# RWKV-7 chunk systems: the scales go into the inverse itself, and the groups of systems are regrouped

## The chip, the cores and the metric

The kernel runs on one core of one Trainium2 chip. The metric is the device time of one execution in microseconds, the median of several runs. TensorE (PE, with its weight loads as PEld), VectorE (DVE), ScalarE (ACT) and GpSimd (POOL) each work off their own queue of instructions in order, and SyncE (SP) issues all DMAs from one queue, also in order.

## The reference, cut to what matters

Two layers run over 1104 token rows (64 sample rows and 1040 prompt rows): a gated DeltaNet layer, then an RWKV-7 layer. The change touches the RWKV-7 layer only, whose state update is

```python
kk = l2norm((k * k_k).reshape(B, T, H, N))
b_h = kk * a_h
S = (S * d_t[:, :, None, :]
     + jnp.einsum('bhvk,bhk->bhv', S, -kk_t)[..., None] * b_t[:, :, None, :]
     + v_t[..., None] * k_t[:, :, None, :])
```

The kernel computes it in chunks of 64 rows. Within a chunk the steps form a unit lower triangular system of 64 x 64, and its inverse is needed for every chunk and head. With the keys not normalised, the system is I + L D, where the diagonal D holds 1 / |key|^2 (plus 1e-6) of each row. What is stored for the later stage is D times the inverse, transposed as the matmuls need it.

## The kernel before, in words

Layer 0 comes first; its inverses of 8 groups also go through `inverse32` (72 partitions, diagonal of ones). Layer 1 has three parts: `keys_decay_rate` projects keys, decay and rate and stores them in DRAM (cakd); then `layer1` loops over 24 weight tiles (r, v and z; `project`) while the systems are inverted; then the wave, which runs the recurrence.

There are 24 items (a pair of heads by a segment of 384 columns), six chunks in each. `rwkv_inverse(b)` is called five times, within the loop behind the tiles 0, 3, 6, 9 and 12. It first prepares its items one by one (L1246 to L1291): the load of cakd into sldcak, ScalarE, VectorE and POOL scaling it, the store of abd, 24 small matmuls for the system (fL), copied by ScalarE into the diagonal blocks GD (L1274) and the lower left block L21 (L1276), and the squared norms (frss), transposed by VectorE (L1290) with 1e-6 added (L1291) into rk. Then come, for the whole group at once: the reciprocal (L1294), its transposition (bblk, L1296), the transposition of GD into invA (L1299) and its multiplication by bblk (L1300). `inverse32` eliminates 31 times, with two VectorE instructions each (L448 and L450), on a tile invT that POOL has set to the unit matrix (L442 and L443). Two transpositions make T1n (L1306) and the upper half of sTD (L1307). All of this has the same size whatever the count of items in the group.

Then `inverse_merge` runs for each item: 12 matmuls on either half of the partitions (mY: L21 by T1n), VectorE multiplying the result by rk on its way out of PSUM into invY (L465, two instructions), 12 matmuls on either half (mU), and ScalarE writing the negated result into sTD (L62). POOL multiplies the item's part of sTD by rk (L1312), and six DMAs (L1315 and L1317) write it to ttd in DRAM. Of these six, two write zeros: the upper right quarter of each inverse, which is zero from a memset at the first group (L1305).

The wave loads the inverse of an item with one DMA of 128 x 384 (rTT, L1331), when it prepares that item.

The framework arranges the instructions of this stage on all engines by a simulated timeline, so a change of one instruction shifts others past each other; in the wave only TensorE's order is written out by hand. Projections have the tile d on TensorE; their weights come by DMA (wraw), ScalarE makes whi (L86), POOL makes wlo (L90). The mixed inputs of the projections are xa, xc, xh and xl (ScalarE, VectorE and POOL).

Of the kernel before, what the change touches and what calls it, by code (L numbers as in the profile page):

```python
# [35 lines left out]
class Builder:  # L36
# [401 lines left out]
    def inverse32(self, A, nb, pool):  # L438
# [4 lines left out]
        nc.gpsimd.memset(T[:, 0:1024:33], 1.0)  # L443
# [8 lines left out]

    def inverse_merge(self, L21, TT, T1n, scale_col, pool, th0, n):

        nc = self.nc
        pY = self.ps("m", 2, "Y")
        yv = pY[:, 0:32 * n].rearrange("p (c i) -> p c i", i=32)
        for c in range(n):
            for p in (0, 1):
                a = 64 * p  # L460
                self.mm(yv[a + 32:a + 64, c, :], L21[a:a + 32, th0 + c, :], T1n[a:a + 32, th0 + c, :])
        Y = self.t(pool, [128, 192], "invY", 2)[:, 0:32 * n].rearrange("p (c i) -> p c i", i=32)
        for p in (0, 1):
            a = 64 * p + 32
            nc.vector.tensor_tensor(Y[a:a + 32], yv[a:a + 32],  # L465
                                    scale_col[a:a + 32].unsqueeze(2).broadcast_to([32, n, 32]), op=ALU.mult)
        pU = self.ps("m", 2, "U")
        uv = pU[:, 0:32 * n].rearrange("p (c i) -> p c i", i=32)
        for c in range(n):
            for p in (0, 1):  # L470
                a = 64 * p
                self.mm(uv[a:a + 32, c, :], Y[a + 32:a + 64, c, :], TT[a + 32:a + 64, c, 0, :])
        for p in (0, 1):
            a = 64 * p
            self.act(TT[a:a + 32, :, 1, :], uv[a:a + 32], AF.Identity, scale=-1.0)


# [681 lines left out]
    def rwkv_masks(self, ap, first=False):  # L1159
# [14 lines left out]
        if first:  # L1174
# [11 lines left out]
            nc.gpsimd.memset(self.GD[:, :, 30:32], 0.0)  # L1186
# [18 lines left out]
    def rwkv_open(self):  # L1205
# [4 lines left out]
        self.ttd, self.abd = self.dram([24, 128, 384], "ttd"), self.dram([24, 128, 768], "abd")  # L1210
# [28 lines left out]
    def rwkv_inverse(self, b, pool):  # L1239

        items = range(5 * b, min(5 * b + 5, 24))
        nc, t = self.nc, self.t
        rk2, L21, GD, TD = self.rk2[:, b], self.L21[b % 2], self.GD, self.TD
        for q, n in enumerate(items):
# [46 lines left out]
            nc.vector.tensor_scalar(rk2[:, C], nt[:, :, 0], 1e-6, None, op0=ALU.add)  # L1291
        if len(items) < 5:
            nc.gpsimd.memset(GD[:, :, 6 * len(items):30], 0.0)
# [14 lines left out]
        for q, n in enumerate(items):  # L1308
# [5 lines left out]
            for a in (0, 64):  # L1314
                nc.sync.dma_start(d[a:a + 32], TT[a:a + 32])  # L1315
                for x in (0, 1):
                    nc.sync.dma_start(d[a + 32:a + 64, :, x], TT[a + 32:a + 64, :, 1 - x])  # L1317
# [639 lines left out]
```

## Time and profile before

| what | us |
|---|---|
| median of three runs (2352.32 to 2361.63) | 2361.1 |
| the profiled execution | 2359.64 |
| its span | 2357.9 |
| its mean granted TensorE clock | 0.967 |
| first load of an item (sldcak) | 1471.0 |
| first mY of the first group | 1571.7 |
| first mY of the last group | 1817.2 |
| last write of ttd is issued | 1844.4 |

All places are us from the start of the span. A row of groups gives line, engine, operation, tiles written and read, shapes and count, then the busy time, the mean ns of one, and the idle time of the engine ahead of it with what ended that. A row of waits gives the waiting instruction, what it waited for, and the sum, the count and the longest. L90 and L62 are helpers' lines, so the tile names matter there. A line number in the profile is one of the kernel before; the changed kernel's numbers differ by a few.

### The profile page before, as it was taken

The numbers are of one execution on the slowest core, as the hardware profiler recorded it, in microseconds if no ns is written. First come the engines' busy times: TensorE is split into PE (matmuls) and PEld (weight loads), VectorE is DVE, ScalarE is ACT, GpSimd is POOL, SyncE is SP. The second block draws the span as 40 slices with busy tenths as digits, with TensorE's granted clock in tenths as the row PEclk, the third lists the DMA queues.
The fourth block names the chain that finished last, engine by engine and source line by source line (L and its number), as shares of the span: only waits on it lengthen the run. The fifth ranks groups of instructions, "written<-read, shape, count | busy, mean of one in ns | idle before, by whom it ended". The sixth has DMA issues, their size and how long they took to land. (4 is left out here: it accounts for less than half of the span.)

```text
span 2357.9 us, 55429 instructions
## 1 busy us (share of the span) xinstructions
PE 2159.2 (92%) x20452; PEld 1959.9 (83%) x20452; DVE 1592.9 (68%) x4248; ACT 1284.4 (54%) x3642; POOL 932.5 (40%) x1268
## 2 busy tenths in 40 slices
PE   6989999999999999999999999888888998899886
PEld 5888988888898989888989999777778876678775
DVE  6868678685867686784335833589988366667755
ACT  5455646564655555557333745647435355577763
POOL 3435334443434343344231623535334433344433
PEclk9999999999999999999999999999899999999998
DMA  3424333323333333336153154554543655677654
GB/s 113 106 69 111 88 85 81 107 66 102 90 90 94 88 112 88 84 97 194 49 160 86 46 178 161 164 152 133 172 113 89 188 151 144 178 218 227 212 161 129
DMA packets 434744, 293.37 MB, mean 124 GB/s; under 512 B 148729, under 2 KB 417642, under 8 KB 434474
## 3 DMA queue, kind: packets, MB, share of 16 engines
q1 hardware_dynamic: 434474, 289.84, 42.6%
q8 instruction: 161, 2.64, 0.5%
q14 instruction: 109, 0.89, 0.1%
HBM read 202.74 MB, written 87.00 MB: 123 GB/s over the span
## 5 line engine op out<-in xcount | busy, mean ns | idle before, releaser
L90 POOL TENSOR_TENSOR wlo<-wraw,whi 128x512 fp32r<-128x512 f32 (+2 forms) x252 | 329.6, 1310 | 351.0 <-ACT whi L86 325.8
L76 PE MATMUL d<-xc,whi 128*128 128x384 f32 (+2 forms) x910 | 261.7, 344 | 7.6 <-DVE xc L90 2.6
L86 ACT CAST whi<-wraw 128x512 fp32r<-128x512 f32 (+2 forms) x252 | 151.7, 603 | 128.9 <-PE dq L76 50.5
L415 DVE SCALAR_TENSOR_TENSOR cvy<-raw,cw,cvy 128x408 f32<-128x408 f32 (+2 forms) x288 | 178.3, 632 | 15.8 <-ACT cvy L62 13.9
L448 DVE TENSOR_TENSOR invtmp<-invA,invT 72x31 f32<-72x31 f32 (+31 forms) x403 | 173.2, 430 | 11.1 <-DMA invA<-ltd 5.1
L76 PEld LDWEIGHTS d<-xc,whi 128*128 128x128 f32 (+1 forms) x910 | 168.6, 192 | 14.3 <-issue 3.2
L450 DVE TENSOR_TENSOR invT<-invT,invtmp 72x31 f32<-72x31 f32 (+31 forms) x403 | 169.7, 421 | 6.5
L76 PE MATMUL dz<-xc,whi 128*128 128x384 f32 (+1 forms) x480 | 149.5, 343 | 0.0
L76 PE MATMUL d<-xa,whi 128*128 128x384 f32 (+3 forms) x450 | 143.0, 350 | 4.2 <-DVE xa L90 1.7
L76 PE MATMUL dv<-xc,whi 128*128 128x384 f32 (+1 forms) x480 | 146.7, 334 | 0.0
L76 PE MATMUL d<-xc,wlo 128*128 128x384 f32 (+2 forms) x428 | 142.7, 342 | 1.4 <-POOL wlo L90 1.3
L815 POOL TENSOR_SCALAR Sb<-Sb,eglb 128x128 f32<-128x128 f32 x128 | 80.4, 646 | 89.2 <-DMA Sb<-in_state_gdn 34.1
L76 PE MATMUL dv<-xa,whi 128*128 128x384 f32 (+1 forms) x288 | 100.3, 348 | 0.1
L76 PE MATMUL dz<-xa,whi 128*128 128x384 f32 (+1 forms) x288 | 100.3, 348 | 0.0
L76 PEld LDWEIGHTS d<-xa,whi 128*128 128x128 f32 (+1 forms) x450 | 83.7, 191 | 10.9 <-issue 2.7
L76 PEld LDWEIGHTS dz<-xc,whi 128*128 128x128 f32 x480 | 89.6, 192 | 0.8
L76 PEld LDWEIGHTS dv<-xc,whi 128*128 128x128 f32 x480 | 88.6, 188 | 0.5 <-issue 0.4
L76 PE MATMUL d<-xa,wlo 128*128 128x384 f32 (+3 forms) x252 | 86.7, 344 | 2.1 <-POOL wlo L90 2.1
L76 PE MATMUL d<-xh,whi 128*128 128x384 f32 (+1 forms) x256 | 84.1, 343 | 4.1 <-ACT xh L86 4.0
L62 ACT ACTIVATE o<-rA,gcol 128x128 f32<-128x128 f32 x128 | 46.6, 372 | 72.5 <-DVE S L726 72.0
L76 PE MATMUL d<-xl,whi 128*128 128x384 f32 (+1 forms) x256 | 84.0, 345 | 2.1 <-DVE xl L90 2.0
L76 PE MATMUL d<-xh,wlo 128*128 128x384 f32 (+1 forms) x256 | 83.8, 342 | 1.7 <-POOL wlo L90 1.7
(512 smaller groups left out, 7025.6 us busy)
## 6 DMA issues: line engine op xcount, KB each, us to landing
wraw<-in_gdn_w_in SPq DMA_DIRECT2D x96, 256.0 KB
wraw<-in_rwkv_w_rkvz SPq DMA_DIRECT2D x80, 256.0 KB
Sb<-in_state_gdn SPq DMA_DIRECT2D x64, 256.0 KB
sldcak<-cakd SPq DMA_DIRECT2D x24, 576.0 KB
fldcak<-cakd SPq DMA_DIRECT2D x24, 576.0 KB
cakd<-ev SPq DMA_DIRECT2D x56, 192.0 KB
wraw<-in_rwkv_w_o SPq DMA_DIRECT2D x40, 256.0 KB
E<-drow SPq DMA_DIRECT2D x24, 384.0 KB
```

The source lines that it names most:

```text
L62: return self.nc.scalar.activation(out, in_, func, bias=bias, scale=scale, **kw)
L76: self.nc.tensor.matmul(out, lhsT, rhs, start=start, stop=stop)
L86: nc.scalar.copy(hi, x)
L90: e.tensor_tensor(lo, x, hi.bitcast(F32), op=ALU.subtract)
L415: nc.vector.scalar_tensor_tensor(y[:, 0:wd], raw[:, k:k + wd], cw[k], y[:, 0:wd], op0=ALU.mult, op1=ALU.add)
L448: nc.vector.tensor_tensor(tmp, A[:, j, j + 1:32].unsqueeze(2).broadcast_to([nb, n, m]), Tv[:, j, 0:m].unsqueeze(1).broadcast_to([nb, n, m] ...
L450: nc.vector.tensor_tensor(Tv[:, j + 1:32, 0:m], Tv[:, j + 1:32, 0:m], tmp, op=ALU.subtract)
L815: nc.gpsimd.tensor_scalar(Sb[:, u], Sb[:, u], self.eglb[:, hv, 4 * g + u:4 * g + u + 1], None, op0=ALU.mult)
```

## The change

The diagonal D goes into the start of the elimination: POOL copies bblk to the diagonal of invT where ones stood, so that the inverse comes out already scaled, and nothing has to be scaled afterwards. So the VectorE multiplication of invY becomes a plain copy on ScalarE, and POOL's multiplication of sTD is gone. The addition of 1e-6 goes from VectorE to POOL. The groups are 4, 5, 5, 5 and 5 items where they were 5, 5, 5, 5 and 4; the calls stay at the same tiles. The writes of ttd, six per item, become six per group, in a DRAM tile laid out by group.

```diff
-    def inverse32(self, A, nb, pool):
+    def inverse32(self, A, nb, pool, diag=None):
...
-        nc.gpsimd.memset(T[:, 0:1024:33], 1.0)
+        if diag is None:
+            nc.gpsimd.memset(T[:, 0:1024:33], 1.0)
+        else:
+            nc.gpsimd.tensor_copy(T[:, 0:1024:33], diag)
...
-        for p in (0, 1):
-            a = 64 * p + 32
-            nc.vector.tensor_tensor(Y[a:a + 32], yv[a:a + 32],
-                                    scale_col[a:a + 32].unsqueeze(2).broadcast_to([32, n, 32]), op=ALU.mult)
+        for a in (32, 96):
+            self.nc.scalar.copy(Y[a:a + 32], v[a:a + 32])
...
-            nc.gpsimd.memset(self.GD[:, :, 30:32], 0.0)
+            nc.gpsimd.memset(self.GD[:, :, 24:32], 0.0)
...
-        self.ttd, self.abd = self.dram([24, 128, 384], "ttd"), self.dram([24, 128, 768], "abd")
+        self.ttd, self.abd = self.dram([5, 128, 1920], "ttd"), self.dram([24, 128, 768], "abd")
...
-        items = range(5 * b, min(5 * b + 5, 24))
+        items = range(max(5 * b - 1, 0), 5 * b + 4)
...
-            nc.vector.tensor_scalar(rk2[:, C], nt[:, :, 0], 1e-6, None, op0=ALU.add)
-        if len(items) < 5:
-            nc.gpsimd.memset(GD[:, :, 6 * len(items):30], 0.0)
+            nc.gpsimd.tensor_scalar(rk2[:, C], nt[:, :, 0], 1e-6, None, op0=ALU.add)
...
-        Tv = self.inverse32(A.rearrange("p i s -> p s i"), 128, pool)
+        Tv = self.inverse32(A.rearrange("p i s -> p s i"), 128, pool, blk)
...
-        for q, n in enumerate(items):
-            TT = TD[:, 6 * q:6 * q + 6]
-            self.inverse_merge(L21, TT, T1n, rk2[:, 6 * q:6 * q + 6], pool, 6 * q, 6)
-            v = TT.rearrange("p c x i -> p c (x i)")
-            nc.gpsimd.tensor_tensor(v, v, rk2[:, 6 * q:6 * q + 6].unsqueeze(2).broadcast_to([128, 6, 64]), op=ALU.mult)
-            d = self.ttd[n].rearrange("p (c x i) -> p c x i", x=2, i=32)
-            for a in (0, 64):
-                nc.sync.dma_start(d[a:a + 32], TT[a:a + 32])
-                for x in (0, 1):
-                    nc.sync.dma_start(d[a + 32:a + 64, :, x], TT[a + 32:a + 64, :, 1 - x])
+        for q in range(len(items)):
+            C = slice(6 * q, 6 * q + 6)
+            self.merge_right(self.merge_left(L21[:, C], T1n[:, C], pool), TD[:, C])
+        w = 6 * len(items)
+        d = self.ttd[b].rearrange("s (c x i) -> s c x i", x=2, i=32)[:, 0:w]
+        for a in (0, 64):
+            nc.sync.dma_start(d[a:a + 32], TD[a:a + 32, 0:w])
+            for x in (0, 1):
+                nc.sync.dma_start(d[a + 32:a + 64, :, x], TD[a + 32:a + 64, 0:w, 1 - x])
```

`merge_left` holds the mY matmuls and the copy, `merge_right` the mU matmuls and the negated write to sTD; both are otherwise the old `inverse_merge`. The wave's load of rTT takes its 384 columns out of the group's 1920. Up to the first load of an item the order of the instructions is the same on every engine, and in the wave TensorE's order is the same too.

The order shows the change at three places. First VectorE, behind the first elimination of all, where the first group is merged. Before:

```order
L1307 STREAM_TRANSPOSE sTD_18165<-invT_18669 128x32x32
L1264 TENSOR_TENSOR sldcak_19407<-sldcak_19407 128x384
L1258 TENSOR_TENSOR sldcak_19455<-sldcak_19455 128x383
L465 TENSOR_TENSOR invY_18783<-mY_18770,rk_3193_18162 32x192 x2
L1299 STREAM_TRANSPOSE invA_19503<-sGD_18164 128x1024
L1290 STREAM_TRANSPOSE rkc_19497<-frss_19492 128x192
L465 TENSOR_TENSOR invY_18821<-mY_18808,rk_3193_18162 32x192 x2
L1291 TENSOR_SCALAR rk_3193_18162<-rkc_19497 128x6
L1264 TENSOR_TENSOR sldcak_19455<-sldcak_19455 128x384
L1294 RECIPROCAL rk_3193_18162<-rk_3193_18162 128x32
L1296 STREAM_TRANSPOSE bblk_19501<-rk_3193_18162 128x32
L1300 TENSOR_TENSOR invA_19503<-invA_19503,bblk_19501 128x1024
```

The same place on VectorE with the change:

```order
L1305 STREAM_TRANSPOSE sTD_18165<-invT_18617 128x32x32
L1258 TENSOR_TENSOR sldcak_19295<-sldcak_19295 128x383
L1290 STREAM_TRANSPOSE rkc_19341<-frss_19336 128x192
L1264 TENSOR_TENSOR sldcak_19295<-sldcak_19295 128x384
L1258 TENSOR_TENSOR sldcak_19347<-sldcak_19347 128x383
L1297 STREAM_TRANSPOSE invA_19395<-sGD_18164 128x1024
L1290 STREAM_TRANSPOSE rkc_19389<-frss_19384 128x192
L1264 TENSOR_TENSOR sldcak_19347<-sldcak_19347 128x384
L1292 RECIPROCAL rk_3193_18162<-rk_3193_18162 128x32
L1294 STREAM_TRANSPOSE bblk_19393<-rk_3193_18162 128x32
L1298 TENSOR_TENSOR invA_19395<-invA_19395,bblk_19393 128x1024
L1258 TENSOR_TENSOR sldcak_19949<-sldcak_19949 128x383
```

The invY rows and the addition into rk are gone from VectorE, and its reciprocal now follows an addition on POOL. In both orders the last two items of the second group are prepared here.

Second SP, at the start of the stage, where the first two items have just been loaded. Before:

```order
L1221 DMA sldcak_18406<-cakd 128x3x384
L1150 DMA cakd<-ev_18143 128x336
L1110 DMA rvd<-ev_18342 128x384
L1110 DMA rvd<-ev_18370 128x384
L1265 DMA abd<-sldcak_18401 128x768
L1221 DMA sldcak_18458<-cakd 128x3x384
```

The same place on SP with the change:

```order
L1110 DMA rvd<-ev_18342 128x384
L1314 DMA ttd<-sTD_18165 32x24x32
L1314 DMA ttd<-sTD_18165 960x1x32
L1314 DMA ttd<-sTD_18165 32x24x32
L1314 DMA ttd<-sTD_18165 960x1x32 x7
L1110 DMA rvd<-ev_18370 128x384
```

The ten writes of zeros, two for each of the five groups, have moved ahead of the whole stage. The other writes of ttd stand behind each group's merges, in two pairs.

Third TensorE, at the first merge of the last group (mY), among projections (d). Before:

```order
L76 MATMUL d_22959<-xc_107,whi_22949 128x384 x2
L76 MATMUL d_22959<-xc_107,wlo_22950 128x384
L76 MATMUL mY_22161<-T1n_22158,L_3196_18166 32x32 x12
L76 MATMUL d_22959<-xc_107,whi_22949 128x384 x2
L76 MATMUL d_22959<-xc_107,wlo_22950 128x384
```

The same place on TensorE with the change:

```order
L76 MATMUL d_22820<-xl_2814_15536,whi_22816 128x384
L76 MATMUL d_22849<-xc_107,wlo_22811 128x384
L76 MATMUL d_22849<-xc_107,whi_22810 128x384 x2
L76 MATMUL mY_22013<-T1n_22010,L_3196_18166 32x32 x12
L76 MATMUL d_22849<-xc_107,wlo_22811 128x384
```

Here mY stands later among the projections: 232 of their matmuls came behind it, up to the first one of the wave's gate (zz), and 206 come now.

36 lines of the change are left out of this document (17 added, 19 removed).

## The prediction

> **What bounds the kernel now.** I read the page first, then the busy time in stretches, then the waits of TensorE in the stretch that the change touches. The page's head says which engine is the fullest.
>
> ```profile
> span 2357.9 us, 55429 instructions
> ...
> PE 2159.2 (92%) x20452; PEld 1959.9 (83%) x20452; DVE 1592.9 (68%) x4248; ACT 1284.4 (54%) x3642; POOL 932.5 (40%) x1268
> ```
>
> TensorE (PE) is busy 92% of the span, so anything that does not make TensorE wait less, or run at a higher clock, is worth nothing. The edits lie in one stage: the systems are inverted while the r, v and z projections run. The stretches around it (columns: PE, PEld, DVE, ACT and POOL busy us with counts, granted clock, DMA share, GB/s):
>
> ```profile
> 1420.00:1473.00 53.00, 50.68 (x286) 48.97 (x284) 22.07 (x31) 31.07 (x66) 17.40 (x22) 0.97 0.47 157
> 1473.00:1500.00 27.00, 21.23 (x135) 16.80 (x135) 17.99 (x30) 21.27 (x49) 16.92 (x27) 0.81 0.35 115
> 1500.00:1540.00 40.00, 38.72 (x471) 35.72 (x470) 20.05 (x37) 21.20 (x52) 17.61 (x36) 1.00 0.60 185
> 1540.00:1680.00 140.00, 118.29 (x1569) 104.37 (x1568) 128.85 (x271) 76.06 (x185) 59.98 (x68) 0.91 0.49 143
> 1680.00:1817.00 137.00, 118.93 (x1399) 106.81 (x1397) 126.73 (x248) 63.01 (x146) 57.86 (x56) 0.95 0.43 123
> 1817.00:1864.00 47.00, 46.81 (x427) 45.63 (x428) 16.60 (x32) 14.99 (x33) 19.21 (x37) 0.96 0.67 197
> ```
>
> From 1540 to 1817 VectorE (DVE) is busy 128.85 + 126.73 = 255.6 of 277 us, or 92%, and TensorE only 237.2: it idles 39.8 us and is granted a clock of 0.91 and 0.95. Before and behind that stretch DVE is half empty and TensorE full. So here DVE is the bound, or very near it. The waits of TensorE in that stretch say the same (us in total, times, longest):
>
> ```profile
> PE mY L76 <- DVE T1n L1306: 7.1, 4, 2.0
> PE fL L76 <- DVE sldcak L1264: 6.1, 4, 1.9
> PE d L76 <- POOL wlo L90: 3.4, 4, 1.2
> PE mU L76 <- DVE invY L465: 3.2, 3, 1.1
> ...
> PE d L76 <- DVE xc L90: 2.6, 1, 2.6
> ...
> PE fL L76 <- DVE invtmp L448: 2.4, 1, 2.4
> ...
> PE d L76 <- DVE xl L90: 2.0, 2, 1.2
> ...
> PE fL L76 <- DVE invT L450: 0.4, 1, 0.4
> ```
>
> The seven rows that name DVE hold 7.1 + 6.1 + 3.2 + 2.6 + 2.4 + 2.0 + 0.4 = 23.8 us, that is 0.60 of the 39.8 us. That share is my rate of exchange below: of a microsecond taken off DVE here, TensorE gets 0.60 back. It is the choice that matters most; its ends are 0 (the chain goes through ScalarE or the DMAs instead) and 1 (DVE alone sets the pace).
>
> **What leaves DVE.** Two groups of instructions go to other engines. In 1540 to 1817 (busy us, mean ns, idle before):
>
> ```profile
> L465 DVE TENSOR_TENSOR invY<-mY,rk 32x192 f32<-32x192 f32 x40 | 14.3, 357 | 5.7 <-PE mY L76 4.6
> ...
> L1291 DVE TENSOR_SCALAR rk<-rkc 128x6 f32<-128x6 f32 x19 | 5.7, 300 | 0.1
> ```
>
> That is 14.3 + 5.7 = 20.0 us. The 31 elimination steps are neither fewer nor shorter: a group of four items costs as much as one of five.
>
> **What leaves POOL, and what that is to DVE.** The multiplication of the finished blocks (L1312) is gone: 24 instructions in the whole stage.
>
> ```profile
> L1312 POOL TENSOR_TENSOR sTD<-sTD,rk 128x384 f32<-128x384 f32 x24 | 21.6, 899 | 55.8 <-ACT sTD L62 45.8 <-DMA ttd<-sTD 7.1 <-DMA sldcak<-cakd 2.8
> ...
> L1259 POOL COPY sldcak<-sldcak 128x6 f32<-128x6 f32 x24 | 6.4, 268 | 58.0 <-DVE sldcak L1258 51.9 <-DVE invtmp L448 5.6 <-POOL m_blocks L1179 0.5
> ```
>
> POOL is under half full, so its 21.6 us alone buy nothing. But DVE is stretched beside it: of each shape here, one instruction beside an L1312 and one without.
>
> ```profile
> 1590.43 0.83 POOL L1312 TENSOR_TENSOR sTD<-sTD,rk 128x384 f32<-128x384 f32 x1 [3.91 <-ACT sTD L62]
> ...
> 1595.64 0.98 POOL L1312 TENSOR_TENSOR sTD<-sTD,rk 128x384 f32<-128x384 f32 x1
> ```
> ```profile
> 1590.88 0.60 DVE L450 TENSOR_TENSOR invT<-invT,invtmp 128x192 f32<-128x192 f32 x1
> ...
> 1595.96 0.92 DVE L448 TENSOR_TENSOR invtmp<-invA,invT 128x240 f32<-128x240 f32 x1
> ```
> ```profile
> 1562.89 0.36 DVE L450 TENSOR_TENSOR invT<-invT,invtmp 128x192 f32<-128x192 f32 x1
> ...
> 1613.18 0.41 DVE L448 TENSOR_TENSOR invtmp<-invA,invT 128x240 f32<-128x240 f32 x1
> ```
>
> The stretch is 0.60 - 0.36 = 0.24 and 0.92 - 0.41 = 0.51, 0.37 us on the mean. With 40 invY in the stretch there are 20 such multiplications: 20 x 0.37 = 7.4 us. The ends are 0 and 20 x 0.899 = 18.0 us. *By the Trainium skill ("SBUF — State Buffer", section "Who interferes with whom") a VectorE instruction with two SBUF inputs and a GpSimd instruction that reads SBUF exclude each other for the whole instruction, which would return up to the 18.0 us and give an estimate near 2335 us. The two rows agree that there is a stall, but show only about half of it.*
>
> **What is added.** POOL gets the 24 additions of 1e-6 (128x6; the POOL copy of that shape, L1259, takes 268 ns) and the five diagonals: 6.4 + 1.3 us against 21.6 removed. New is that DVE now waits for POOL twice in a group: its reciprocal for the last addition, and its first elimination step for the copied diagonal. Behind DVE's waiting instruction stands the whole elimination. Each wait is bounded by 0 and by one POOL weight split ahead in the queue (L90 takes 1.34 us at 1592.10, quoted below); the second is covered by the 128x1024 multiplication between the transposed scales and the first step. Of 10 such waits I take 3 us in all; the ends are 0 and 13.
>
> ```profile
> 1592.10 1.34 POOL L90 TENSOR_TENSOR wlo<-wraw,whi 128x512 fp32r<-128x512 f32 x1 [0.84 <-ACT whi L86]
> ```
>
> ScalarE (ACT) gets the 48 copies out of PSUM. It has such a copy already, and the second half of each merge:
>
> ```profile
> L62 ACT ACTIVATE sTD<-mU 32x192 f32<-32x192 f32 x48 | 15.4, 320 | 23.1 <-PE mU L76 22.8
> ...
> L1276 ACT COPY L<-fL 32x192 f32<-32x192 f32 x48 | 14.8, 307 | 0.4
> ```
>
> At 307 ns they are 14.7 us; ACT is busy 139 of the 277 us, so I cost them at nothing. Their cover is that free half. The hop from mY to mU gets no longer (2 x 0.307 against 2 x 0.357). If the cover fails, see the third rival.
>
> **SP and the DMAs.** 144 writes of ttd become 30. Ten of them are the zero quarters, which no longer wait for any merge: the order puts them ahead of everything, at about 1473, in a place where SP stands still now.
>
> ```profile
> 1473.01 10.17 SPq L1110 DMA_DIRECT2D rvd<-ev  x2
> ...
> 1494.63 0.52 SPq L1221 DMA_DIRECT2D sldcak<-cakd  x1
> 1495.25 1.01 SPq L198 DMA_DIRECT2D wraw<-in_rwkv_w_rkvz  x1
> ```
> ```profile
> L1317 SPq DMA_DIRECT2D ttd<-sTD x96: 549/596/1477, 1581.4 to 1844.4; - x96
> L1315 SPq DMA_DIRECT2D ttd<-sTD x48: 308/537/879, 1580.9 to 1843.2; - x48
> ```
>
> A write of 192 runs takes SP 0.596 us, one of 32 runs 0.537, and the load at 1494.63 of 384 runs 0.52: the count of runs does not show. Ten are then 6 us within the wait of 10, and free. SP loses about 144 x 0.58 - 30 x 0.6 = 66 us of issuing, but I credit nothing: TensorE waits for a weight split on POOL only 3.4 us in the stretch. The bytes and runs are the same.
>
> **The tail.** Behind the first mY of the last group stand 232 projection matmuls in the old order and 206 in the new, so once DVE has the last transposed inverse, less is left. TensorE starts one each 0.176 us (nine single ones in a row, the first and the last: 1.41 us for eight steps):
>
> ```profile
> 1859.06 0.34 PE L76 MATMUL d<-xh,whi 128*128 128x384 f32 x1
> ...
> 1860.47 0.34 PE L76 MATMUL d<-xl,whi 128*128 128x384 f32 x1
> ```
>
> 26 x 0.176 = 4.6 us less, and one more item to merge. The tail has 47 us, of which 232 x 0.176 = 40.8 are projections; the other 6.2 us for four items make about 1.5 each at most, 1.1 if the lower clock takes its part. So -4.6 + 1.1 = -3.5 us.
>
> **The sum.** Off DVE come 20.0 + 7.4 - 3.0 = 24.4 us; at 0.60 that is 14.6 us for TensorE. With the tail: 14.6 + 3.5 = 18.1 us. The profiled execution took 2359.6 us, 1.7 more than its span, and lies 1.5 under the median of the three runs (2361.1), inside their spread. 2359.6 - 18.1 = **2341.5 us**. The head (groups of four, then fives) I cost at nothing: TensorE is 38.72 of 40 us full while the first group is prepared.
>
> **The rivals.**
> - *DVE alone sets the pace, and the clock follows.* The whole 24.4 us come off, and the waits that vanish spare slow periods too:
>
> ```profile
> 1573.00:1577.00 4.00, 2.83 (x60) 1.89 (x61) 3.58 (x7) 1.53 (x5) 2.67 (x5) 0.79 0.56 160
> 1577.00:1582.00 5.00, 5.00 (x58) 4.50 (x58) 3.05 (x8) 1.49 (x4) 1.83 (x2) 0.50 0.84 264
> ```
>
>   Right behind the first group's waits TensorE has a clock of 0.50 for 5 us, a loss of 2.5 us. With two such periods gone: 24.4 + 3.5 + 5 = 32.9, 2326.7 us. For it: DVE at 92%. Against: 16.0 us of TensorE's idle time is not DVE's. *The Trainium skill ("TensorE: Matmul & The Clock Gate", "What's actually happening") puts the drop to half clock behind an idle window of about 3.4 us; by that rule shorter waits would leave the clock alone and the sum stay as it is. The trace differs: the longest wait in the stretch is 2.6 us, and the clock halves.* Chance 0.14.
> - *The wait stays and only its name changes.* The last elimination still ends when TensorE has no other work placed ahead, since the order places mY anew. Then only the wait for invY (3.2 us) and the tail (3.5) are saved: 2353 us. Chance 0.20.
> - *ScalarE becomes the in-order blocker; slower.* It now stands twice in each merge behind TensorE's small matmuls. Today the one place costs it 22.8 us of waiting (row of sTD above); a second like it is 22.8 more, behind which stand the weight casts, the evictions of d and the mixing. If all of it reaches TensorE: + 22.8 - 3.2 - 3.5 = + 16.1, 2375.7 us. It decides from the point where such a wait is longer than ScalarE's free time around it, and that is 277 - 139 = 138 us for the 20 items of the stretch, 6.9 us each. Against: 22.8 / 24 is under 1 us. Chance 0.12.
> - *The change does not do what it says at the head*: the ten zero writes, each with 768 or 960 runs, take SP in proportion, 5 x 0.596 = 3 us each. 30 us against a gap of 10 hold the third sldcak load and the weights 20 us: 2361 us. Against: the rows of 384 runs. Chance 0.06.
>
> **How the numbers follow.** Forecast 0.48 (its own range 2332 to 2349), larger gain 0.14: faster by over 0.5% 0.62. Within 0.5%, about what a measurement of this kernel can tell from no change, 0.26 (second and fourth rival). Slower 0.12. The range runs from 2320, near the end of the larger gain with the POOL stall at its upper end, to 2363, which holds the rivals without a gain and leaves the slower one out.
>
> **What would show it.** Right: DVE busy falls by about 25 us from 1540 on with the counts of invY and rk gone from it; the last mY comes 12 to 20 us earlier; TensorE's waits for DVE shrink from 23.8 to about 10 us. Wrong: waits of TensorE on ScalarE (whi, xh, invY) in their place; DVE waiting for rk or the diagonal by more than 1 us a group; a gap on TensorE between 1485 and 1540 with SP busy on ttd. If DVE shrinks as said and the end does not move, my 0.60 was wrong.

## The result, and the profile after

The changed kernel takes 2352.45 us (median) where the kernel before takes 2361.14. The ratio is 0.9969, 95% interval 0.9956 to 0.9983: 7.3 us faster, 4.0 to 10.4. The forecast was 18.1 us, so the direction was right and the gain less than half. Below, a ratio is always to the kernel before, and times and differences go by it (the two medians alone lie 8.7 us apart); 0.001 is 2.36 us, and a range behind a difference of two kernels combines their two intervals (root of the sum of squares).

The page's head, changed kernel (profiled execution 2353.39 us):

```profile
span 2351.5 us, 55207 instructions
...
PE 2157.2 (92%) x20452; PEld 1959.8 (83%) x20452; DVE 1570.0 (67%) x4176; ACT 1298.2 (55%) x3690; POOL 922.5 (39%) x1267
```

VectorE lost 22.9 us of 1592.9, ScalarE gained 13.8, POOL lost 10. Of the stretches that the prediction showed, the four up to the last merges, now of the changed kernel:

```profile
1473.00:1500.00 27.00, 20.42 (x124) 16.48 (x124) 18.83 (x31) 21.41 (x46) 16.64 (x28) 0.87 0.61 153
1500.00:1540.00 40.00, 40.00 (x443) 37.51 (x442) 25.21 (x44) 23.30 (x57) 20.85 (x38) 1.00 0.60 187
1540.00:1680.00 140.00, 124.45 (x1639) 112.03 (x1638) 125.05 (x246) 85.51 (x211) 62.31 (x81) 0.95 0.51 157
1680.00:1817.00 137.00, 116.01 (x1402) 104.93 (x1402) 111.73 (x210) 69.12 (x167) 49.34 (x51) 0.94 0.39 114
```

In 1540 to 1817 VectorE is busy 125.05 + 111.73 = 236.8 us, 18.8 less than before: the relief came. TensorE was busy 237.2 us there and is now 240.5: it idles 36.5 us where it idled 39.8. VectorE idles 40.2 us there where it idled 21.4, and TensorE got 3.3 us of that.

A fixed stretch cuts the two kernels at different points of their work, so the measure from here on is the whole stage, from the first load of an item to the first matmul of the wave's gate. It holds the same 4004 matmuls in every kernel. Before, then changed:

```profile
1471.00:1863.60 392.60, 345.58 (x4003) 310.70 (x4003) 309.92 (x612) 198.50 (x468) 173.47 (x225) 0.93 0.49 144
```
```profile
1477.20:1857.70 380.50, 338.20 (x4005) 306.82 (x4004) 288.44 (x539) 212.25 (x513) 163.01 (x226) 0.95 0.49 147
```

The stage is 12.1 us shorter. The changed kernel entered it 6.2 us later in its profiled execution (1477.2 against 1471.0), in a part whose order is the same, which is why the two profiled executions lie only 6.2 us apart; one profile of the stage is uncertain by some microseconds too. It is also more than the 4.0 to 10.4 us that all executions show. How TensorE's time in it changed can be read off: its idle time went from 392.60 - 345.58 = 47.0 us to 42.3, and its busy time for the same matmuls from 345.58 to 338.20, because its loss to a lowered clock, estimated as length times (1 - clock), went from about 27 us to about 19. **In these two profiles the larger part came by way of the clock, the smaller by way of idle time**; the run y_eps_dve below has as short a stage and splits the other way.

VectorE's busy time in the stage fell by 21.5 us, and 12.1 / 21.5 = 0.56 looks like the 0.60 of the prediction. But the two numbers only stand side by side; what VectorE's time is worth has to be measured by changing it alone.

TensorE's waits in 1540 to 1817, changed kernel:

```profile
PE mY L76 <- DVE T1n L1304: 10.1, 5, 3.4
PE fL L76 <- DVE sldcak L1264: 7.6, 5, 2.2
PE d L76 <- POOL wlo L90: 4.6, 4, 2.1
...
PE fL L76 <- DVE invT L453: 1.8, 2, 1.6
PE mU L76 <- ACT invY L465: 1.8, 2, 1.1
PE fL L76 <- DVE invtmp L451: 1.7, 1, 1.7
PE d L76 <- DVE xc L90: 1.6, 1, 1.6
PE d L76 <- DVE xl L90: 1.4, 2, 0.8
```

The six rows that name DVE hold 24.2 us; seven rows held 23.8 before, and the prediction wanted about 10 in their place. The wait for T1n was 7.1 us and is 10.1; that for sldcak was 6.1 and is 7.6. The wait of mU for invY shrank, from 3.2 (for VectorE) to 1.8 (for ScalarE). So VectorE did 18.8 us less here, and TensorE waited for it as long as before. VectorE's own waits in the same stretch, before and then changed:

```profile
DVE sldcak L1258 <- ACT sldcak L62: 5.9, 6, 2.5
DVE invY L465 <- PE mY L76: 4.6, 3, 1.8
...
DVE invA L1299 <- ACT sGD L1274: 0.3, 1, 0.3
```
```profile
DVE invA L1297 <- ACT sGD L1274: 11.9, 4, 7.7
DVE sldcak L1258 <- ACT sldcak L62: 11.5, 3, 6.6
DVE sldcak L1264 <- POOL sldcak L1263: 4.8, 4, 2.0
...
DVE rk L1292 <- POOL rk L1291: 0.4, 1, 0.4
```

A new row stands at the top: the transposition that opens a group's elimination now waits for the last item's blocks (sGD). The worst one in time, VectorE first, then ScalarE:

```profile
1753.85 1.25 DVE L1297 STREAM_TRANSPOSE invA<-sGD 128x1024 f32<-128x1024 f32 x1 [7.70 <-ACT sGD L1274]
```
```profile
1752.15 0.65 ACT L62 ACTIVATE sTD<-mU 32x192 f32<-32x192 f32 x2 [5.23 <-PE mU L76]
1752.83 0.65 ACT L465 COPY invY<-mY 32x192 f32<-32x192 f32 x2
1753.50 0.32 ACT L1274 COPY sGD<-fL 128x192 f32<-128x192 f32 x1
```

ScalarE waits 5.23 us for TensorE's mU, and the copy of sGD that VectorE needs stands behind it and behind the new copy of Y.

### The profile page after: what moved, and what is told of

Read it like the earlier page. It is cut to its first block, busy times and chain, and to the rows that moved or that the text cites. A ratio compares the mean times of both kernels' runs of the same rounds, so it can differ in the third digit from the quotient of the medians.

```text
span 2351.5 us, 55207 instructions
## 1 busy us (share of the span) xinstructions
PE 2157.2 (92%) x20452; PEld 1959.8 (83%) x20452; DVE 1570.0 (67%) x4176; ACT 1298.2 (55%) x3690; POOL 922.5 (39%) x1267
## 5 line engine op out<-in xcount | busy, mean ns | idle before, releaser
L451 DVE TENSOR_TENSOR invtmp<-invA,invT 72x31 f32<-72x31 f32 (+31 forms) x403 | 165.3, 410 | 12.5 <-DMA invA<-ltd 5.4
L62 ACT ACTIVATE attn<-attn,gcol 128x128 f32<-128x128 f32 x144 | 46.6, 390 | 71.8 <-POOL attn L526 71.7
```

The lines of the kernel that those rows point to most:

```text
L62: return self.nc.scalar.activation(out, in_, func, bias=bias, scale=scale, **kw)
L451: nc.vector.tensor_tensor(tmp, A[:, j, j + 1:32].unsqueeze(2).broadcast_to([nb, n, m]), Tv[:, j, 0:m].unsqueeze(1).broadcast_to([nb, n, m] ...
```

## The experiments

**Theories.** *0*: the prediction's price, 0.60 us for each microsecond of VectorE, holds, and another part of the change eats the gain. *1*: preparation of the items sets the pace, so VectorE's freed time becomes idle. *2*: TensorE's fixed order only renames its waits. Later came four candidates for what carries the gain: *3* (VectorE's place in the merges, not its time), *4* (SyncE's queue), *5* (the groups) and *6* (POOL's multiplication).

### What is VectorE's time worth?

**dve_plus**, **before_dve_plus**: ahead of each merge, in the changed kernel and in the one before,

```diff
+            for _ in range(3):
+                nc.vector.tensor_tensor(self.dz, self.dz, self.dz, op=ALU.mult)
```

> The changed kernel with three more VectorE instructions per item (128x160, on a scratch tile that nothing else reads; 72 in all), issued where an item's merge stands; nothing waits for them but VectorE's own queue. About 0.33 us each by the 128x192 row of before (0.36 us), so 24 us in all and 20 us in the stretch in which the groups are eliminated: about what the change took off VectorE. Theory 0 (the 0.60 of the prediction holds, and another part of the change eats the gain): VectorE time costs the end 0.60, so 12 us slower than the changed kernel (2364 us, ratio to the kernel before about 1.002). Theory 1 (VectorE is no longer what the stage waits for; a group's elimination waits for its items to be prepared): the new instructions fill VectorE's idle 39.9 us of the stretch, and the time stays within 4 us of the changed kernel (ratio 0.997). Theory 2 (TensorE's order is fixed by the simulated timeline, and the waits only change names): also within 4 us, and TensorE's waits for T1n stay at 7 to 10 us.

> The kernel before with the same three added VectorE instructions per item (24 us in all, 20 in the stretch, where VectorE was busy 92% and idle 21 us). Theory 0: 0.60 a microsecond, 12 us slower than before (ratio 1.005). If VectorE is the full bound there: 20 us slower (1.0085). Theories 1 and 2 as far as they hold for the kernel before too: under 5 us (1.002), because its waits too are for preparation and placement.

Measured: 1.0004 (0.9986 to 1.0023) and 1.0058 (1.0034 to 1.0082). The runs missed their place. In dve_plus the added instructions alone (VectorE is the third of the busy columns):

```profile
1473.00:1500.00 27.00, 0.00 (x0) 0.00 (x0) 11.65 (x29) 0.00 (x0) 0.00 (x0) 0.85 0.51 123
1500.00:1540.00 40.00, 0.00 (x0) 0.00 (x0) 16.99 (x39) 0.00 (x0) 0.00 (x0) 0.99 0.57 174
1540.00:1680.00 140.00, 0.00 (x0) 0.00 (x0) 0.00 (x0) 0.00 (x0) 0.00 (x0) 0.91 0.50 155
```

Nothing held them, so the framework put all of them ahead of the eliminations, and 31 us in front of the first group cost 8 and 14 us. They price VectorE at the head, not in the stretch.

**elim_plus**, **before_elim_plus**: the dose (the added work) tied to its place, in `inverse32` behind the subtraction,

```diff
+            if diag is not None and j % 2 == 0 and j < 30:
+                nc.vector.tensor_tensor(self.dz, T[:, 0:160], T[:, 0:160], op=ALU.mult)
```

(before: `nb == 128` in place of `diag is not None`).

> The dose of the run dve_plus, now tied to its place: the changed kernel with 15 more VectorE instructions in each of the five eliminations (128x160, reading the tile that the step before has written, so that they cannot move to another place). At the 0.41 us that the same instruction took in the run dve_plus they are 6 us a group, 25 us over the four groups of the stretch. Theory 0 (0.60): 15 us slower than the changed kernel (2367 us, ratio 1.003). Theory 1 (preparation sets the pace of the elimination, VectorE has slack): under 5 us slower (2357 us or less, ratio under 0.999), and invA's wait for sGD (11.9 us) shrinks by most of the added time. Theory 2 (TensorE's waits are renamed by its placement): also under 5 us, with invA's wait for sGD as it was.

> The kernel before with 15 more VectorE instructions in each of the five eliminations (25 us over the stretch), tied to their place as in the run elim_plus, where they cost 1.2 us. Before the change VectorE was busy 92% of the stretch, idle 21 of 277 us. Theory 0 (VectorE's time is the pace before the change, at the 0.60 of the prediction): 15 us slower than before (ratio 1.0064). Full bound: up to 25 us (1.0106). Theory 3 (what TensorE waits for in the stretch is VectorE's place in the merges, invY between mY and mU in VectorE's queue, and not VectorE's time): under 5 us (ratio under 1.002).

The added instructions over the whole stage, changed kernel and kernel before:

```profile
1465.10:1850.60 385.50, 0.00 (x0) 0.00 (x0) 27.65 (x75) 0.00 (x0) 0.23 (x1) 0.92 0.48 144
```
```profile
1465.70:1863.20 397.50, 0.00 (x0) 0.00 (x0) 32.86 (x75) 0.00 (x0) 0.23 (x1) 0.92 0.48 141
```

Measured: 0.9974 (0.9956 to 0.9991), that is 1.2 us slower than the change (4 faster to 6 slower) for 27.7 us of VectorE, and 1.0033 (1.0013 to 1.0052), 7.8 us slower than before (3 to 12) for 32.9 us. The price of a microsecond is about 0.04 with the change (at most 0.23) and 0.24 without it (0.09 to 0.37). The two are not clearly apart: both profiled stages are 5 us longer than without the dose. But 0.60 would be 17 and 20 us, outside both ranges, so theory 0 falls. In elim_plus invA's wait for sGD is 8.1 us over the stage where it was 11.9, which lies between what theories 1 and 2 said.

**half_elimination**:

```diff
-        for j in range(31):
+        for j in range(0, 31, 1 if diag is None else 2):
```

> The changed kernel with every second of the 31 elimination steps of the RWKV systems left out (16 stay; the output is not the reference's). That takes half of the 135.7 us of L451 and L453 off VectorE in the stretch, 68 us, and leaves all else. Theory 0: 0.60 x 68 = 41 us, capped by what TensorE has to win there (33 us idle and half of 37 us at half clock): 30 to 40 us faster than the changed kernel (2312 to 2322 us, ratio about 0.982). Theory 1: preparation sets the pace, so under 10 us (2343 us or more, 0.993 or more), and the wait of invA for sGD grows from 11.9 to over 30 us. Theory 2: 10 to 20 us, since the simulated timeline places the merges earlier as well; TensorE still waits 6 to 10 us for T1n.

Measured: 0.9929 (0.9903 to 0.9956), 9.4 us (2 to 17) less than the change, with 16 of the 31 elimination steps of each group left and the others left out. The stage:

```profile
1472.30:1847.90 375.60, 344.21 (x4003) 311.81 (x4003) 226.41 (x392) 213.57 (x517) 159.75 (x225) 0.93 0.51 154
```

VectorE's busy time fell by 62.0 us (288.44 to 226.41), so a microsecond was worth 0.15 (0.04 to 0.27). TensorE idles 31.4 us instead of 42.3, but takes 344.21 us for its matmuls instead of 338.20, at a lower clock: over half of the idle time won was lost again. VectorE meets other waits: in the stage that for ScalarE's part of the preparation grew from 21.2 us to this,

```profile
DVE sldcak L1258 <- ACT sldcak L62: 39.6, 15, 5.5
```

while that for sGD, which theory 1 wanted above 30 us, is 5.1. The last group's first mY came at 1787.5, 315.2 us into the stage (337.6 in the change), and yet the stage was only 4.9 us shorter. The projection matmuls behind that mY, half_elimination and then the changed kernel (first busy column: TensorE, tile d alone):

```profile
1787.50:1847.90 60.40, 56.40 (x303) 54.32 (x303) 7.72 (x14) 6.36 (x13) 0.97 0.62 190
```
```profile
1814.80:1857.70 42.90, 38.82 (x206) 37.01 (x206) 4.91 (x9) 3.90 (x8) 0.96 0.59 173
```

An earlier inverse only moves projections behind it: 303 instead of 206. What counts is how long TensorE idles, or runs slow, until then.

**y_eps_dve**: the changed kernel with the instructions of the prediction's 20 us back on VectorE (the first as a plain copy),

```diff
-            self.nc.scalar.copy(Y[a:a + 32], v[a:a + 32])
+            self.nc.vector.tensor_copy(Y[a:a + 32], v[a:a + 32])
-            nc.gpsimd.tensor_scalar(rk2[:, C], nt[:, :, 0], 1e-6, None, op0=ALU.add)
+            nc.vector.tensor_scalar(rk2[:, C], nt[:, :, 0], 1e-6, None, op0=ALU.add)
```

> The changed kernel as it is (ratio 0.9969), without the priority, and the copy of Y and the addition of 1e-6 back on VectorE: the 20.0 us of the prediction's step on what leaves VectorE, and nothing else. By that step 20 x 0.60 = 12 us slower (ratio 1.002). By the dose elim_plus (25 us cost 1.2): within 3 us (ratio 0.9955 to 0.998). By the dose before_elim_plus (0.31 a microsecond): 6 us slower (ratio 0.9995).

```profile
1469.90:1850.00 380.10, 341.63 (x4004) 309.56 (x4004) 303.66 (x611) 196.65 (x466) 155.76 (x202) 0.94 0.50 147
```

Measured: 0.9946 (0.9929 to 0.9963), 5.4 us (0 to 11) *faster* than the change. VectorE's 303.66 us are 15.2 more than the change's 288.44, and the stage is as long (380.1): 12.5 us shorter than before with only 6.3 us less on VectorE. Here 8.5 us of that are TensorE's idle time and 4.0 its busy time. Moving these instructions off VectorE brought nothing, if anything a small loss. A row of VectorE's waits, 1540 to 1817, suggests why: the wait for sGD, 11.9 us in the change, is almost gone.

```profile
DVE invA L1297 <- ACT sGD L1274: 0.6, 2, 0.4
```

So with the copies of Y on ScalarE, VectorE seems to have spent what it saved waiting for ScalarE to hand over sGD; here it stands 13.4 us for mY instead. The order of the other instructions differs as well, so this link is a reading of the two profiles and not shown by itself.

### Is it preparation?

**prepare_first**, **before_prepare_first**: the loop over the items (body indented, otherwise as it was) gets priority, so that the framework places its instructions ahead of others that are ready, in the changed kernel and in the one before,

```diff
+        with self.tc.high_priority():
         for q, n in enumerate(items):
```

> The changed kernel with the preparation of the items (the loop ahead of the reciprocal) given priority over all else in the order, so that its steps on ScalarE, POOL, TensorE and SP stand ahead of merges, weight splits and projections that are ready in the same place. Nothing is computed otherwise. Theory 1: the waits of invA for sGD (11.9 us) and of L1258 for ScalarE (11.5 us) go, and with them 5 to 12 us of the time (2340 to 2347 us, ratio 0.992 to 0.995). Theory 0: VectorE's load is the same, so the time stays within 4 us. Theory 2: TensorE's order changes at random places, within 4 us either way.

> The kernel before with the preparation of the items given priority in the order, as in the run prepare_first (2336.8 us, 0.9917), and nothing of the change. Theory 1: before the change VectorE is full (92%), so earlier preparation finds no VectorE time: 0 to 6 us faster than before (ratio 0.9975 to 1.0), and the change is then worth 16 us or more once preparation is out of its way. If the priority is worth the same whatever VectorE's load: 12 us faster than before (ratio 0.995), and the change stays worth 7 us. Theory 2: the order of TensorE is dealt anew, within 5 us either way.

Measured: 2336.8 us, 0.9917 (0.9889 to 0.9946), and 2360.87 us, 0.9999 (0.9982 to 1.0016). So the priority is worth 12 us (5 to 20) with the change and nothing before it, as theory 1 had it, and with the priority the change is worth 19 us (12 to 27). VectorE's waits in prepare_first, 1540 to 1760; the row for sGD is gone and that for ScalarE is down from 11.5:

```profile
DVE sldcak L1259 <- ACT sldcak L62: 4.1, 6, 1.8
DVE mixs L1025 <- ACT mixs L62: 1.9, 2, 1.7
```

The stage, prepare_first and then before_prepare_first:

```profile
1470.90:1837.80 366.90, 334.79 (x4005) 310.42 (x4004) 285.42 (x543) 213.78 (x517) 163.76 (x230) 0.93 0.53 158
```
```profile
1470.70:1858.40 387.70, 338.02 (x4004) 311.28 (x4004) 313.26 (x615) 199.62 (x469) 178.53 (x231) 0.93 0.50 149
```

TensorE idles 32.1 us in the one and 49.7 in the other. In the latter its longest rows, 1540 to 1801:

```profile
PE mY L76 <- DVE T1n L1307: 12.7, 5, 4.1
PE mU L76 <- DVE invY L465: 10.2, 6, 3.8
```

**first_elim_plus**, **first_half_elim**: the diffs of elim_plus and of half_elimination on prepare_first.

> The changed kernel with preparation given priority (prepare_first, 2336.8 us) and the 15 added VectorE instructions in each elimination of the run elim_plus (25 us over the stretch). Theory 1: with preparation early VectorE is the pace again, so a microsecond of VectorE costs 0.6 or more: 15 us or more slower than prepare_first (2352 us or more, ratio 0.998 or more). Theory 2, and any theory in which VectorE has slack in general: under 5 us slower (ratio under 0.994).

> The changed kernel with preparation given priority and every second elimination step left out (the output is not the reference's), 68 us less of VectorE in the stretch. Without the priority that was worth 9.4 us (half_elimination against the changed kernel). Theory 1: VectorE is the pace here until TensorE is full, so the gain is larger than 9.4: 12 to 22 us faster than prepare_first (2315 to 2325 us, ratio 0.982 to 0.987). Theory 2, or a floor set by TensorE's own work: under 9 us (2328 us or more, ratio 0.988 or more).

Measured: 0.9907 (0.9883 to 0.9932), no slower than prepare_first for the whole dose, and 0.9885 (0.9858 to 0.9912), 7.6 us faster (2 slower to 17 faster) for half the elimination. So the second half of theory 1 falls: with preparation early VectorE does not become the pace again. Theory 2 has the doses right, but it allowed prepare_first 4 us, and that run won 12.

### Which part of the change carries the gain?

**first_y_dve**, **first_y_eps_dve**: the first two lines, and all four, of the diff of y_eps_dve, on prepare_first.

> The changed kernel with preparation given priority (prepare_first, ratio 0.9917), and the copy of Y out of PSUM back on VectorE (a plain copy, two a merge, 48 in all), where the multiplication of invY stood before; the diagonal and the rest of the change stay. Theory 3: TensorE's mU waits for invY in VectorE's queue again, as in before_prepare_first (10.2 us in six waits), and the time goes up by 8 to 15 us (2345 to 2352 us, ratio 0.995 to 0.998). Theory 0 (VectorE's time): 14 us on VectorE at 0.60 are 8.6 us too, but with no waits of mU for invY; since first_elim_plus cost nothing for 25 us, this theory now gives 0. Neither, if another part of the change carries the 19 us between before_prepare_first and prepare_first: within 4 us of prepare_first.

> The changed kernel with preparation given priority, and both groups of instructions that left VectorE back on it (the copy of Y and the addition of 1e-6), 20 us in the stretch; POOL's multiplication stays away. The prediction's step: 20 x 0.60 = 12 us slower than prepare_first (ratio 0.997). Theory 3: as first_y_dve (0.993), or up to 0.997 if the short addition, on which a group's reciprocal waits, is late in VectorE's queue as well. Theory 6: 0.993 or less, what is left belonging to POOL.

Measured: 0.9930 (0.9907 to 0.9953), 3 us slower than prepare_first (6 faster to 12 slower), and 0.9908 (0.9884 to 0.9931), 2 us faster (11 faster to 7 slower). Theory 3 falls.

**first_writes_item**, on prepare_first:

```diff
             self.merge_right(self.merge_left(L21[:, C], T1n[:, C], pool), TD[:, C])
-        w = 6 * len(items)
-        d = self.ttd[b].rearrange("s (c x i) -> s c x i", x=2, i=32)[:, 0:w]
+            d = self.ttd[b].rearrange("s (c x i) -> s c x i", x=2, i=32)[:, C]
```

with the six DMAs of `TD[..., C]` inside the loop.

> The changed kernel with preparation given priority (ratio 0.9917), and the writes of ttd item by item again, six DMAs each (144 in all where the change has 30). Theory 4 (SyncE's queue carries the gain: 66 us of issuing less, and loads and weights no longer behind writes that wait for a merge): 8 us or more slower than prepare_first (ratio 0.995 or more), with ScalarE's waits for the loads of sldcak above 34 us. Theory 3, and the prediction, which credited nothing to SyncE: within 4 us (ratio 0.990 to 0.9935).

**first_regroup_back**, on prepare_first:

```diff
-        items = range(max(5 * b - 1, 0), 5 * b + 4)
+        items = range(5 * b, min(5 * b + 5, 24))
```

> The changed kernel with preparation given priority (ratio 0.9917), and the groups 5, 5, 5, 5 and 4 again. By the prediction's steps the head is worth nothing and the tail 3.5 us: 3 to 4 us slower (ratio 0.993). Theory 5 (the short first group carries the gain: the first elimination starts one item, about 10 us, earlier, and all behind it follows): 8 to 12 us slower (ratio 0.995 to 0.997). Theory 3: as the prediction, under 5 us.

Measured: 0.9903 (0.9885 to 0.9922) and 0.9900 (0.9879 to 0.9922). With the priority neither costs anything by itself, and theories 4 and 5 fall there.

**first_pool_back**, **change_pool_back**: behind each merge, on prepare_first and on the changed kernel,

```diff
+            v = TD[:, C].rearrange("p c x i -> p c (x i)")
+            nc.gpsimd.tensor_tensor(v, v, self.one6.unsqueeze(2).broadcast_to([128, 6, 64]), op=ALU.mult)
```

**first_all_back**: this and the diff of y_eps_dve together, on prepare_first.

> The changed kernel with preparation given priority (ratio 0.9917, and 0.990 to 0.991 in the three runs that undid a part without cost), and POOL multiplying each finished item of sTD again as before the change, by a tile of ones: 24 instructions of 128x384, 21.6 us on POOL, between the merge and the write. Theory 6 (POOL's multiplication carries the gain: it stretches VectorE and keeps sTD, and with it the next group, waiting): 10 us or more slower (ratio 0.995 or more). The prediction's own step (7.4 us of stretch on VectorE at 0.60): 4.4 us slower (0.993). Theory 3 (VectorE's place in the merges): within 3 us (0.992 or less).

> The changed kernel with preparation given priority, and all three back: Y and 1e-6 on VectorE and POOL's multiplication (by ones). What stays of the change is the diagonal in the start of the elimination, the groups and the writes. If these three carry the 20 us, in whatever shares: as before_prepare_first, ratio 0.998 to 1.0. If the two runs beside this one add up to it, each part counts for itself; if both lie near 0.992 and this one near 1.0, either relief is enough and the last one to go costs. If this one stays under 0.995, the groups and writes count after all, together with something else.

> The changed kernel (ratio 0.9969), without the priority, with POOL multiplying each finished item of sTD again (by ones; 24 instructions of 128x384). Theory 6 (POOL's multiplication carries the gain): 6 to 9 us slower, ratio 0.9995 to 1.001. The prediction's step on POOL (7.4 us of stretch on VectorE at 0.60 are 4.4 us): ratio 0.9988. If it counts only together with the priority: within 3 us, ratio 0.9955 to 0.998.

Measured: 0.9945 (0.9923 to 0.9968), 7 us slower than prepare_first (2 faster to 15 slower); 0.9952 (0.9928 to 0.9975), which is 10 us (3 to 18) slower than first_y_eps_dve; and 1.0036 (1.0022 to 1.0051), which is 16 us (11 to 21) slower than the change. With POOL's 24 multiplications back the change is no gain at all. The stage of change_pool_back, and POOL's wait for merges in it (1500 to 1865):

```profile
1472.00:1864.80 392.80, 344.35 (x4003) 311.31 (x4002) 295.12 (x539) 212.04 (x513) 184.26 (x251) 0.93 0.48 142
```
```profile
POOL sTD L1312 <- ACT sTD L62: 37.0, 14, 9.1
```

VectorE is stretched by 295.12 - 288.44 = 6.7 us, about what the prediction put down (7.4), and such time is worth 0.04 to 0.24 by the doses, under 3 us even at the upper end of their ranges. POOL also stands still 37.0 us for merges, up to 9.1 at a time, with the weight splits and the copies of the preparation behind it in its queue.

**before_diagonal**: that part alone, on the kernel before,

```diff
-            self.inverse_merge(L21, TT, T1n, rk2[:, 6 * q:6 * q + 6], pool, 6 * q, 6)
-            v = TT.rearrange("p c x i -> p c (x i)")
-            nc.gpsimd.tensor_tensor(v, v, rk2[:, 6 * q:6 * q + 6].unsqueeze(2).broadcast_to([128, 6, 64]), op=ALU.mult)
+            self.inverse_merge(L21, TT, T1n, self.one6, pool, 6 * q, 6)
```

and the diagonal in `inverse32`, as in the change.

> The kernel before with the diagonal in the start of the elimination and POOL's multiplication gone, and nothing else of the change: VectorE still multiplies invY (by ones, at the same place and in the same shape) and adds 1e-6, the groups are 5, 5, 5, 5 and 4, the writes go item by item. Theory 6: all of the gain, 6 to 9 us faster than before (ratio 0.996 to 0.9975). The prediction's step on POOL: 4.4 us (0.998). Theory 0 or 3 (the gain is VectorE's): under 2 us (0.999 to 1.001).

```profile
1472.50:1865.50 393.00, 349.28 (x4004) 315.22 (x4003) 308.39 (x614) 197.65 (x467) 158.13 (x207) 0.92 0.50 147
```
```profile
SPq L1318 <- ACT sTD L62: 22.2, 13, 4.5
```

Measured: 1.0014 (0.9994 to 1.0035), no gain. So theory 6 holds only half: putting the multiplication back takes the gain away, and taking it out alone brings none. SyncE now stands 22.2 us for the merges where POOL stood (the second row, 1500 to 1865). Between this kernel and y_eps_dve, 16 us apart, lie the groups, the writes by group, and a plain copy of Y in place of its multiplication, all of it still on VectorE.

## Why the prediction was wrong, point by point

- **The bound (VectorE at 92%, the busiest engine of a stretch in which TensorE idles): read wrongly.** A busy share is no price. The tied dose cost 0.24 us a microsecond in the very kernel in which VectorE was 92% busy.
- **What leaves VectorE, 20.0 us: right in size, wrong in worth.** Put back into the changed kernel it costs nothing (y_eps_dve); no run took it alone out of the kernel before.
- **The stretch beside POOL, 7.4 us: right where it was measured alone** (6.7 us in change_pool_back). In the change the two elimination lines, 310 instructions over the stage, got 4.7 us shorter (148.2 to 143.5), but VectorE's busy time in 1540 to 1817 fell by 18.8 us and not by 20.0 + 7.4. Other instructions grew longer: L1264, for one, went from 548 to 647 ns on the mean (the two rows, 1540 to 1817, before and then changed).

```profile
L1264 DVE TENSOR_TENSOR sldcak<-sldcak 128x384 f32<-128x384 f32 x18 | 9.9, 548 | 0.0
```
```profile
L1264 DVE TENSOR_TENSOR sldcak<-sldcak 128x384 f32<-128x384 f32 x19 | 12.3, 647 | 4.8 <-POOL sldcak L1263 4.8
```

The prediction's "only about half" goes by the whole L1312. The two VectorE instructions met only its last 0.38 and 0.66 us (1590.88 and 1595.96 to its ends at 1591.26 and 1596.62), and the 0.24 and 0.51 us are most of that.

- **New waits for POOL, 3 us: 0.4 us.**
- **The exchange rate of 0.60: the step that failed.** The prediction put it as "of a microsecond taken off DVE here, TensorE gets 0.60 back", from the share of TensorE's idle time that is put down to VectorE. That is a share of the waits as they stand; when VectorE gets faster, another wait ends in their place. The share itself shows it: it is 24.2 of 36.5 us, or 0.66, with VectorE relieved. The tied doses and half_elimination show 0.04, 0.24 and 0.15 instead of 0.60, and putting the moved instructions back cost nothing. Of the 14.6 us that TensorE should have won, the profile shows 3.3 us of idle time in the stretch and 4.7 in the whole stage. By the profiles, what VectorE saved in the stretch became its own waiting: its waits for ScalarE's and POOL's part of the preparation (the rows of sGD and sldcak) went from 6.2 to 28.2 us.
- **The tail, 3.5 us: met by its number and wrong as a term.** It went from 46.4 to 42.9 us. But it is no gain of its own: half_elimination has a tail of 60.4 us in a shorter stage.
- **ScalarE at nothing: right for the copies, doubtful for their cover.** The 40 copies in the stretch cost it 12.5 us (next row). The third rival's 16 us did not come, but sGD now stands behind such copies, and VectorE's 11.9 us of waiting for it are about what it had saved; without the copies they are 0.6.

```profile
L465 ACT COPY invY<-mY 32x192 f32<-32x192 f32 x40 | 12.5, 312 | 5.8 <-PE mY L76 4.9
```

- **SyncE and the head at nothing: not refuted.** TensorE is 40.00 of 40 us full from 1500 to 1540, and the ten writes of zeros fit the gap (next row: 9.24 us; 6 were estimated). The first mY comes 88.4 us into the stage, 100.7 before, but the run that undoes the groups lost nothing.

```profile
1480.06 9.24 SPq L1314 DMA_DIRECT2D ttd<-sTD  x10
```

- **The clock, left to a rival: it carried more than half of what the stage won** in the change's profile (7.4 of 12.1 us), and a third in that of y_eps_dve (4.0 of 12.5).
- **The signs:** the counts of invY and rk went as said, and the last mY comes 8.6 us earlier in the stage (337.6 where it was 346.2; 12 to 20 were wanted).

What came was nearest to the second rival, "the wait stays and only its name changes" (2353 us): T1n is waited for longer than before, and the wait for sGD is new. That its number was met is luck: of its two terms, putting invY back on VectorE costs nothing, and the tail is no gain of its own.

**What stays open.** The change's 7 us are not a sum of its parts. Putting POOL's multiplication back costs 7, 10 and 16 us in three kernels; taking it out of the kernel before brings none. Whether POOL's standing in its queue or the stretch does the harm was not separated, nor were the groups and the writes undone one by one without the priority. Which part carries the change's 7 us therefore stays open; shown is that it stays when most of VectorE's time is put back. Each kernel also has its own order on all engines; the six with the priority that differ by a part without a clear effect (prepare_first, first_elim_plus, first_y_dve, first_y_eps_dve, first_writes_item, first_regroup_back) lie between 0.9900 and 0.9930, so up to 7 us may be the order's own and the measurement's.

The priority on preparation gives the best versions: prepare_first, 2336.8 us, beats both, the kernel before by 20 us and the changed one by 12, and the runs built on it that lie as low are not told apart from it.

## What to carry to other kernels

A share of busy time or of waits tells which engine to look at, not what a microsecond on it is worth: add a dose of work that cannot move away from its place, and read the price before counting on it. Where every engine has an in-order queue, look at what an engine *stands* for (POOL: 45.8 us for merges in a row already quoted) and not only at what it does, and when load is taken off an engine, ask at once what feeds it and let that go first (here 12 us). Count a gain once, as idle and slow time of the full engine over a stage that holds the same work, not as an earlier event plus a shorter tail.

## What the runs showed of the hardware

TensorE's clock can halve around a wait that is short. In the changed kernel TensorE waits once, 2.14 us, ahead of 1616.66, and from 1616.9 the clock is 0.50 for 3.3 us:

```profile
1616.66 0.51 PE L76 MATMUL d<-xa,wlo 128*128 128x384 f32 x1 [2.14 <-POOL wlo L90]
```
```profile
1616.90:1620.20 3.30, 3.30 (x12) 3.30 (x12) 3.23 (x7) 2.18 (x6) 1.27 (x1) 0.50 0.65 187
```

Not every such wait does it: 2.21 us for whi, up to 1798.34, leave the clock at 1.00 from 1796 to 1804. What decides was not found. The costliest case has two waits:

```profile
PE mY L76 <- DVE T1n L1304: 2.5, 1, 2.5
PE fL L76 <- DVE sldcak L1264: 2.0, 1, 2.0
```

The wait of mY ends at 1737.9, that of fL at 1740.5, and within the latter the clock halves for 10.2 us:

```profile
1722.00:1739.80 17.80, 12.97 (x194) 11.71 (x194) 17.08 (x35) 7.59 (x19) 5.39 (x8) 1.00 0.50 158
1739.80:1750.00 10.20, 9.48 (x119) 7.85 (x120) 1.94 (x5) 4.65 (x13) 2.52 (x5) 0.50 0.56 150
```

Between the two waits lie only 0.57 us of small matmuls. 9.48 us of work at half the clock lose 4.7 by estimate, as much as the two waits themselves (4.5). A write of 768 or 960 runs does not take SyncE in proportion either: 20 such writes have a median of 0.658 us (a write of 192 runs took 0.596 before), one of them 2.6; the ten of zeros took 0.92 on the mean.

```profile
L1314 SPq DMA_DIRECT2D ttd<-sTD x20: 318/658/2591, 1480.1 to 1817.1; - x20
```
